# A hybrid decoder layer on one core: modulation pieces used one step after their load

## The chip, the cores and the metric

One core of one Trainium2 chip. The metric is the device time of one launch in microseconds (us), lower is better. The kernel before took 1296.67 us in the median of three runs (1293.77 to 1296.86).

## The reference

One layer of a decoder trunk on 256 tokens of width 2048, all in float32. A conditioning vector `c` gives six modulation vectors by one matrix-vector product; they shift, scale and gate the two sub-layers:

```
mod = (silu(c) @ w_ada + b_ada)                    # w_ada: 2048 x 12288, 96 MB
sh1, sc1, g1, sh2, sc2, g2 = split(mod, 6)
h = rms_norm(x, norm1_g) * (1 + sc1) + sh1
q, k, v, u = split(h @ w_in, ...)                  # w_in: 2048 x 4096
attn = dilated_attention(rms_norm(q), rms_norm(k), v)
y = gelu(s5_mixer(u, ...));  ssm = y * sigmoid(y @ w_glu + b_glu)
x = x + g1 * (concat(rms_norm(attn), rms_norm(ssm)) @ w_out)
h2 = rms_norm(x, norm2_g) * (1 + sc2) + sh2
return x + g2 * (square(relu(h2 @ w_ff1)) @ w_ff2) # w_ff1: 2048 x 8192, w_ff2: 8192 x 2048
```

## The kernel before, in words

**Weights.** Every large product is made in three matmuls of a reduced float32 form (`mm3`, lines 188 to 192): the weight is split into a high part `wh` (a copy on ScalarE, ACT) and a low part `wl` (a subtraction on VectorE, DVE), the activation likewise, and TensorE (PE) adds high by high, high by low and low by high. `load_w` (line 178) loads a block of 512 x 512 weights in two halves of 512 KB, each into one place of the tag `raw` (line 173), splits each and returns both. There are five places `raw` (`RAW = 5`), three `wh` and three `wl`. All loads are issued by one queue, SP, in order; a load waits there until a place of its tag is free, and a `raw` place comes free when the `wl` made from it is done.

**Modulation.** `w_ada` is read in 96 pieces of 1 MB (24 blocks of four). `ada_pieces` (line 238) loads a piece and uses it at once: for the eight blocks in `PE_BLOCKS` by small matmuls on PE (line 246), for the others by a product with a running sum on DVE (`stt`, line 155; two of 128 x 1024 a piece, one for each `raw` place). A piece goes into two `raw` places, or into a place of another tag that is idle at that time: `U`, `PD`, `WB0` (whole, 1 MB) or `T0` (two halves one after the other); `ring["tags"]` names the tags in turn, and `RINGS` holds their lists for six stretches of the program. T0 is also the place of tables and scratch of the state-space part.

**Order.** `pump(n)` (line 276) makes n pieces. `pump_at(i)` adds `PUMPS[i]` to a running sum and pumps the whole part of it; it is called after each part of the input projection (a part is one `load_w` with its 24 matmuls), after each column block of `w_out`, after the first parts of `w_ff1`, and in a few other places; `ff1` pumps one piece at its start, and the last four come in one call before the last `ff2`. `make_h` and `make_h2` need certain pieces to be complete. `PUMPS`, in the order of the program:

```
PUMPS = (2.5, 2.75, 1.0, 1.5, 0.75, 0.75, 1.5, 1.25, 1.0, 2.0, 0.25, 2.75, 1, 0.75)
run(w_in_block(0, [0]), 0) ... n in (6, 7): run(w_in_block(n, [0]), 1)   # kg 0: PUMPS 0, 1
run(w_in_block(2 + w, [0, 1]), 2); run(w_in_pair(4, [0, 1]), 3)          # PUMPS 2, 3
run(w_in_block(0 and 1, [1, 2]), 4); run(w_in_pair(6, [1, 2]), 5)        # PUMPS 4, 5
```

What the program text does not fix is fixed by a planner that runs when the kernel is built (`schedule_with_timeline_sim=True`): for each engine and for SP it takes, at each moment of a modelled run, the instruction that stands earliest in the program among those that could start. So the order on DVE is that in which the model expects loads to land; on the chip each engine then keeps this order.

**Names.** `tc.issue_after(ins)` puts what is traced inside it behind `ins` in the order of its engine, without a wait. A product of a piece is `raw<-raw,cbc` in the trace, a split `wh<-raw` (ACT, L158) and `wl<-raw,wh` (DVE, L133).

Of the kernel before, what the change touches and what calls it, by code (L numbers as in the profile page):

```python
# [1 line left out]

# [7 lines left out]
F32 = mybir.dt.float32  # L10
# [3 lines left out]
ALU = mybir.AluOpType  # L14
PSUM = bass.MemoryType.PSUM

P = 128
# [7 lines left out]
RQ = 4  # L25
NB = 512
RAW = 5
RINGS = (('raw',), ('raw',), ('T0', 'PD', 'raw', 'raw'), ('T0', 'raw', 'raw'), ('U', 'raw'), ('WB0', 'U', 'raw', 'raw'))
PUMPS = (2.5, 2.75, 1.0, 1.5, 0.75, 0.75, 1.5, 1.25, 1.0, 2.0, 0.25, 2.75, 1, 0.75)

COLS = {}
# [11 lines left out]
ADA_ORDER = (4, 0, 5, 1, 6, 2, 7, 3, 8, 9, 10, 11, 12, 16, 13, 17, 14, 18, 15, 19, 20, 21, 22, 23)  # L43
# [70 lines left out]
class _K:  # L114
    def __init__(self, nc, tc, I, out, pools):
        self.nc, self.tc, self.I, self.out = nc, tc, I, out
        self.sb, self.ps = pools
        self.n = 0

    def t(self, tag, shape, dt=F32, bufs=1):  # L120
        self.n += 1
        return self.sb.tile(list(shape), dt, name=f"{tag}_{self.n}", tag=tag, bufs=bufs)

# [4 lines left out]
    def tr(self):  # L128
        self.n += 1
        return self.ps.tile([P, NB], F32, name=f"tr_{self.n}", tag="tr", bufs=4)  # L130
# [7 lines left out]
    def add(self, out, a, b, eng=None):  # L138
        return self.tt(out, a, b, ALU.add, eng)
# [28 lines left out]

    def split(self, hi, lo, v):
        self.copy(hi, v)  # L170
        return self.sub(lo, v, hi.bitcast(F32))

    def raw(self, src, tag="raw"):
        raw = self.t(tag, [P, 2, NB], bufs=RAW if tag == "raw" else 1)
# [13 lines left out]
    def mm3(self, ps, xh, xl, wh, wl, start, stop):  # L188
        mm = self.nc.tensor.matmul
        mm(ps, xh, wh, start=start, stop=False)  # L190
        mm(ps, xh, wl, start=False, stop=False)  # L191
        mm(ps, xl, wh, start=False, stop=stop)  # L192


def _body(nc, tc, I, out, sb, ps):
    k = _K(nc, tc, I, out, (sb, ps))
    t, tr = k.t, k.tr
# [31 lines left out]
    def ada_raw(src):  # L229
        ring["i"] += 1  # L230
        tag = ring["tags"][ring["i"] % len(ring["tags"])]
        if tag not in ("raw", "T0"):
            raw = t(tag, [P, 4, NB])
            nc.sync.dma_start(raw, src.rearrange("p (a n) -> p a n", a=4))
            return [raw]
        return [k.raw(src[:, 2 * NB * i : 2 * NB * i + 2 * NB].rearrange("p (a n) -> p a n", a=2), tag) for i in range(2)]

    def ada_pieces(b):
        c4 = slice(4 * b, 4 * b + 4)
        if b in PE_BLOCKS:  # L240
            acc = tr()
            for g in range(4):
                q = 0
                for raw in ada_raw(I["w_ada"][b, g]):
                    for i in range(raw.shape[1]):
                        mm(
                            acc[32 * q : 32 * q + 32, :], cpad[:, 4 * g + q, :], raw[:, i, :],
                            start=g == 0, stop=g == 3,
                        )
                        q += 1  # L250
                if g < 3:
                    yield
            rows = t("rows", [P, NB], bufs=2)
            copy(rows, acc)
            pc = tr()
            for j in range(4):
                mm(pc[:, j : j + 1], rows[:, 128 * j : 128 * j + 128], ones, start=True, stop=True)
            add(mod[:, c4], pc[:, 0:4], col["b_ada"][:, c4])
        else:
            part = t("adap", [P, 2, 4], bufs=2)  # L260
            for j in range(4):
                o = 0
                for i, raw in enumerate(ada_raw(I["w_ada"][b, j])):
                    n = raw.shape[1] * NB
                    rf = raw.rearrange("p a n -> p (a n)")
                    stt(rf, rf, 1.0, cbc[:, o : o + n], ALU.mult, ALU.mult, accum=part[:, i, j : j + 1])
                    o += n
                if i:
                    add(part[:, 0, j : j + 1], part[:, 0, j : j + 1], part[:, 1, j : j + 1])
                if j < 3:  # L270
                    yield
            add(mod[:, c4], part[:, 0], col["b_ada"][:, c4])
        yield

    state = {"left": 96, "gen": None, "due": 0.0}

    def pump(n=1, until=None):
        while n > 0 and state["left"] > (96 - until if until is not None else 0):
            if state["left"] % 4 == 0:
                state["gen"] = ada_pieces(ADA_ORDER[24 - state["left"] // 4])  # L280
            next(state["gen"])
            state["left"] -= 1
            n -= 1

    # norm1
    rw = t("HB", [P, 4, SEQ])
    onek, sel = rw[:, 3, 0:32], rw[:, 3, P : 2 * P]
    nc.vector.memset(onek, 1.0 / DM)
# [15 lines left out]
    hs = {}  # L304

    def make_h(kg):
        hs[kg] = t("HA" if kg % 2 == 0 else "HB", [P, 2, 4, SEQ], F32R)
        c4 = slice(4 * kg, 4 * kg + 4)
        stt(g1c[:, c4], mod[:, 16 + 4 * kg : 20 + 4 * kg], 1.0, col["n1g"][:, c4], ALU.add, ALU.mult)
        for kc in range(4 * kg, 4 * kg + 4):  # L310
            v = xTf[:, kc]
            mul(v, v, rbc)
            nc.scalar.activation(v, v, AF.Identity, bias=mod[:, kc : kc + 1], scale=g1c[:, kc : kc + 1])
            end = k.split(hs[kg][:, 0, kc % 4], hs[kg][:, 1, kc % 4], v)
        return end.ins
# [152 lines left out]
            pr = slice(64 * gp, 64 * gp + 64)  # L468
            copy(dst(gp)[pr], src[pr])

    # state input tables: rows (s, gp, j), columns (gp, p)
    padB = t("PD", [P, 32, 2, 2, 16])
    padCs = [t(f"WB{i}", [P, 8, 2, 2, 4, 16]) for i in range(2)]
    cw = t("V", [P, 2, 2, 32, 16])
# [26 lines left out]
                nc.tensor.transpose(pt[:, P * e : P * e + P], src, ident)  # L501
            copy(wb[i][:, r : r + 2].rearrange("p r i n -> p (r i n)"), pt)

    # state output tables and the causal kernel inside a chunk
    def ca_step(d, X, Y, rr=slice(0, 32)):
        if d == 0:
            ts(c0[:, 1], c0[:, 1], -1.0, ALU.mult)
# [79 lines left out]

    s5_small()
    pump(8)
    h_end = make_h(0)  # L590
    ring["tags"] = RINGS[0]
    with tc.issue_after(rbc_end):
# [53 lines left out]
    for n in (6, 7):  # L646
        run(w_in_block(n, [3]), 8)

    # attention
    qk = accs["qk"]  # L650
    va = accs["v"]
    qss = t("qss", [P, 4, 32])
# [26 lines left out]
    def y_block(r8):  # L679
        pt = k.acc()  # L680
        pv = pt.rearrange("p (r c) -> p r c", r=8)
        for r in range(r8, r8 + 8):
            mm(pv[:, r - r8], toep[:, r].rearrange("p g s j -> p (g s j)"), u2[:, :, r, :], start=True, stop=False)
            for ri in range(2):
                for gp in range(2):
                    pr = slice(64 * gp, 64 * gp + 64)
                    mm(
                        pv[pr, r - r8], ca[pr, r, ri].rearrange("p s j -> p (s j)"), H[pr, ri, r, :],
                        start=False, stop=ri == 1,
                    )  # L690
        copy(yv[:, :, r8 : r8 + 8], pt.rearrange("p (r h c) -> p h r c", r=8, h=2))

    def att_scores(hp):
# [66 lines left out]
    def row_bcast(b0):  # L760
        g = t("PD", [P, 4, NB])
        for n in range(4):
            pg = tr()
            for j in range(4):
                c = b0 + 4 * n + j
                mm(pg[:, P * j : P * j + P], mod[:, c : c + 1].to_broadcast([P, P]), ident, start=True, stop=True)  # L766
            copy(g[:, n], pg)
        return g
# [59 lines left out]
        att_values(n)  # L828
    branch_rstd(sq2, 2)
    pump(99, until=48)  # L830
    g1b = row_bcast(32)
    x = t("XT", [P, 2, DM])
    nc.sync.dma_start(x, I["x"])

    # w_out
    zs = t("TO", [P, 2, DM])

    def w_out_half(half, xh, xl, n):
# [59 lines left out]

    def make_h2(kg):
        pump(99, until=56 + 8 * kg)  # L900
        c4 = slice(4 * kg, 4 * kg + 4)
        stt(g2c[:, c4], mod[:, 64 + 4 * kg : 68 + 4 * kg], 1.0, col["n2g"][:, c4], ALU.add, ALU.mult)
        for c in range(4 * kg, 4 * kg + 4):
            v = x1T[:, c]
            nc.scalar.activation(v, v, AF.Identity, bias=mod[:, 48 + c : 49 + c], scale=g2c[:, c : c + 1])
            k.split(h2h[:, c], h2l[:, c], v)

    # feed-forward
    y2 = [t("WB2", [P, DM]), t("WB3", [P, DM])]
    slots = [t(s, [P, 2, 4, SEQ], F32R) for s in ("V", "WB0", "HA", "U", "WB1", "HB")]  # L910
    xs = t("XT", [P, 2, 2, 4, SEQ], F32R)
# [68 lines left out]
    for G in range(4):  # L980
        if G < 3:
            aas[G + 1] = [ff1(G + 1, 0)]
        if G == 3:
            pump(99)
            g2b = row_bcast(80)
            for m in range(2):
                mul(y2[m], y2[m], g2b.rearrange("p n f -> p (n f)"))
                add(y2[m], y2[m], z[:, m])
        for n in range(4):
            ff2(G, n, aas[G], G == 3, g2b)  # L990
        if G < 3:
            aas[G + 1] += [ff1(G + 1, j) for j in range(1, 4)]
# [21 lines left out]
```

## Time and profile before

| | |
|---|---|
| runs | 1293.77, 1296.67, 1296.86 us |
| profiled execution | span 1291.1 us from its first to its last instruction; its whole time is not listed beside it, the median of the runs is 5.6 us above the span |
| busy | PE 1210.1, weight loads 947.5, DVE 873.3, ACT 595.8 us |
| read from memory | 296.31 MB, 231 GB/s over the span |

A page's busy shares are averages; the table of stretches (us from the span's start) says where an engine has room. A wait is put down to what ended it. Start times of PE's matmuls are the better measure of their pace, since their ends overlap.

### The profile page before, as it was taken

The page shows a single profiled execution, that of the slowest core. Times are in us where ns is not written, and L with a number is a line of the kernel's source. Part 1 is how long each engine was busy: PE and PEld are TensorE (multiplying, and loading weights), DVE is VectorE, ACT ScalarE, POOL GpSimd, SP SyncE. Part 2 cuts the span into 40 slices and gives each one's busy share as a digit, 9 for nine tenths or more (in the row PEclk, how much of TensorE's full clock was granted, in tenths as well). Part 3 has the DMA queues.
Part 4 walks back from the last instruction along what each step waited for, and adds up shares of the span by engine and source line. Part 5 has one row for each costly group of instructions (what it writes and reads, how often), then busy time and mean ns, then how long its engine had stood idle before and what let it go on. Part 6 is the DMA issues. An engine that isn't in the chain of part 4 may idle for free. (4 is left out here: it accounts for less than half of the span.)

```text
span 1291.1 us, 15788 instructions
## 1 busy us (share of the span) xinstructions
PE 1210.1 (94%) x5818; PEld 947.5 (73%) x5818; DVE 873.3 (68%) x1307; ACT 595.8 (46%) x820; POOL 41.3 (3%) x28
## 2 busy tenths in 40 slices
PE   5787999999999889699999999999999999998998
PEld 1356778866688667477788888888888888886886
DVE  9697678899658988765664456554666555667754
ACT  3579544322388434634454444443344433343432
POOL 3000000000000440000000000000000000000000
PEclk9687999998899999799999999999999999998999
DMA  9687898888726788487555576655667555677562
GB/s 332 234 280 269 332 350 307 291 311 294 260 84 207 239 268 281 156 267 247 193 182 192 189 253 211 217 184 188 224 216 248 185 186 186 224 245 258 176 217 95
DMA packets 80572, 299.44 MB, mean 232 GB/s; under 512 B 8944, under 2 KB 9200, under 8 KB 78576
## 3 DMA queue, kind: packets, MB, share of 16 engines
q1 hardware_dynamic: 80496, 298.45, 68.3%
q8 instruction: 45, 0.74, 0.2%
q14 instruction: 31, 0.25, 0.1%
HBM read 296.31 MB, written 2.10 MB: 231 GB/s over the span
## 5 line engine op out<-in xcount | busy, mean ns | idle before, releaser
L133 DVE TENSOR_TENSOR wl<-raw,wh 128x1024 fp32r<-128x1024 f32 x360 | 443.1, 1234 | 285.4 <-ACT wh L158 283.8
L158 ACT ACTIVATE wh<-raw 128x1024 fp32r<-128x1024 f32 x360 | 380.9, 1060 | 505.4 <-PE acc L192 370.1
L192 PE MATMUL acc<-wh,CA 128*128 128x512 f32 x512 | 204.4, 399 | 0.2 <-DVE CA L133 0.2
L155 DVE SCALAR_TENSOR_TENSOR raw<-raw,cbc 128x1024 f32<-128x1024 f32 x112 | 140.4, 1258 | 59.5 <-DMA raw<-w_ada 57.1
L191 PE MATMUL acc<-wl,TO 128*128 128x512 f32 x448 | 177.4, 396 | 1.4 <-DVE wl L133 1.4
L190 PE MATMUL acc<-wh,TO 128*128 128x512 f32 x448 | 161.9, 395 | 0.9 <-ACT rows L927 0.9
L192 PEld LDWEIGHTS acc<-wh,CA 128*128 128x128 f32 x512 | 97.4, 190 | 22.3 <-DVE CA L133 0.4
L192 PE MATMUL acc<-wh,HA 128*128 128x512 f32 x256 | 101.3, 398 | 0.0
L191 PEld LDWEIGHTS acc<-wl,TO 128*128 128x128 f32 x448 | 84.4, 188 | 21.4 <-DVE wl L133 2.0
L190 PEld LDWEIGHTS acc<-wh,TO 128*128 128x128 f32 x448 | 84.3, 188 | 20.3 <-ACT rows L927 1.1
L191 PE MATMUL acc<-wl,HA 128*128 128x512 f32 x192 | 77.4, 403 | 0.0
L190 PE MATMUL acc<-wh,HA 128*128 128x512 f32 x192 | 71.0, 404 | 6.5 <-ACT wh L158 6.5
L191 PE MATMUL acc<-wl,HB 128*128 128x512 f32 x192 | 76.2, 398 | 0.4 <-DVE wl L133 0.4
L192 PE MATMUL acc<-wh,HB 128*128 128x512 f32 x192 | 75.1, 393 | 0.0
L190 PE MATMUL acc<-wh,HB 128*128 128x512 f32 x192 | 69.8, 399 | 2.2 <-ACT HB L158 2.2
L192 PEld LDWEIGHTS acc<-wh,HA 128*128 128x128 f32 x256 | 48.6, 190 | 11.5 <-DVE T L133 0.8
L191 PE MATMUL acc<-wl,U 128*128 128x512 f32 x128 | 51.0, 398 | 2.5 <-DVE wl L133 2.5
L191 PE MATMUL acc<-wl,WB 128*128 128x512 f32 x128 | 51.4, 402 | 0.0
L192 PE MATMUL acc<-wh,WB 128*128 128x512 f32 x128 | 51.2, 400 | 0.0
L191 PE MATMUL acc<-wl,XT 128*128 128x512 f32 x128 | 50.8, 396 | 0.0
L192 PE MATMUL acc<-wh,XT 128*128 128x512 f32 x128 | 50.7, 396 | 0.0
L190 PEld LDWEIGHTS acc<-wh,HA 128*128 128x128 f32 x192 | 36.4, 191 | 17.5 <-ACT wh L158 9.5
(271 smaller groups left out, 1869.5 us busy)
## 6 DMA issues: line engine op xcount, KB each, us to landing
raw<-w_ff SPq DMA_DIRECT2D x256, 512.0 KB, 4.4
raw<-w_ada SPq DMA_DIRECT2D x158, 512.0 KB, 5.4
raw<-w_in SPq DMA_DIRECT2D x64, 512.0 KB, 5.5
raw<-w_out SPq DMA_DIRECT2D x32, 512.0 KB, 4.8
U<-w_ada SPq DMA_DIRECT2D x8, 1024.0 KB, 7.6
T<-w_ada SPq DMA_DIRECT2D x8, 512.0 KB, 6.2
raw<-w_glu SPq DMA_DIRECT2D x8, 512.0 KB, 5.6
PD<-w_ada SPq DMA_DIRECT2D x3, 1024.0 KB, 6.6
```

The source lines that it names most:

```text
L133: return (eng or self.nc.vector).tensor_tensor(out, a, b, op=op)
L155: self.nc.vector.scalar_tensor_tensor(out, a, s, b, op0=op0, op1=op1, accum_out=accum)
L158: self.nc.scalar.activation(out, a, AF.Copy, scale=scale)
L190: mm(ps, xh, wh, start=start, stop=False)
L191: mm(ps, xh, wl, start=False, stop=False)
L192: mm(ps, xl, wh, start=False, stop=stop)
```

## The change

A piece is now a generator of two steps: the first loads it, the second uses it. `pump` first uses what is pending (`drain`), and then for each of its n pieces again drains, loads the piece and leaves it pending; so of a call with n pieces all but the last are used within the call, and the last one by the next call, whatever its n. A use on DVE is put behind the last split traced so far, a use on PE behind the last main matmul traced so far (`mm3`, and the state output in `y_block`; the GLU's matmuls are not counted). `drain` also runs before a tile of the tags U, PD or WB0 is made, in `make_h` and `make_h2`, and before the two `row_bcast`. T0 is out of `RINGS`.

```diff
+PLACES = ("U", "PD", "WB0")
-RINGS = (('raw',), ('raw',), ('T0', 'PD', 'raw', 'raw'), ('T0', 'raw', 'raw'), ('U', 'raw'), ('WB0', 'U', 'raw', 'raw'))
+RINGS = (('raw',), ('raw',), ('PD', 'raw', 'raw'), ('raw',), ('U', 'raw'), ('WB0', 'U', 'raw', 'raw'))
...
     def t(self, tag, shape, dt=F32, bufs=1):
+        if self.drain and tag in PLACES:
+            self.drain()
...
     def split(self, hi, lo, v):
         self.copy(hi, v)
-        return self.sub(lo, v, hi.bitcast(F32))
+        r = self.sub(lo, v, hi.bitcast(F32))
+        self.last_split = r.ins
+        return r
...
-        mm(ps, xl, wh, start=False, stop=stop)
+        self.last_main = mm(ps, xl, wh, start=False, stop=stop).ins
...
+    def behind(name):
+        ins = getattr(k, name, None)
+        return tc.issue_after(ins) if ins is not None else contextlib.nullcontext()
...
+    def ada_piece(b, g):
         c4 = slice(4 * b, 4 * b + 4)
+        raws = ada_raw(I["w_ada"][b, g])
+        yield
         if b in PE_BLOCKS:
...
+            with behind("last_main"):
+                for raw in raws:
...
+            with behind("last_split"):
+                for i, raw in enumerate(raws):
...
+    pending = []
+
+    def drain():
+        while pending:
+            next(pending.pop(0))
 
     def pump(n=1, until=None):
+        drain()
         while n > 0 and state["left"] > (96 - until if until is not None else 0):
-            if state["left"] % 4 == 0:
-                state["gen"] = ada_pieces(ADA_ORDER[24 - state["left"] // 4])
-            next(state["gen"])
+            drain()
+            i = 96 - state["left"]
+            piece = ada_piece(ADA_ORDER[i // 4], i % 4)
+            next(piece)
+            pending.append(piece)
             state["left"] -= 1
             n -= 1
```

## Rows read from the trace of the kernel before

**Rows 1.** The page's busy time: us, share of the span, instructions.

```profile
PE 1210.1 (94%) x5818; PEld 947.5 (73%) x5818; DVE 873.3 (68%) x1307; ACT 595.8 (46%) x820; POOL 41.3 (3%) x28
```

**Rows 2.** Stretches: length, busy us (count) by engine, clock, DMA share, GB/s.

```profile
60.00:142.00 82.00, 69.17 (x366) 52.89 (x361) 67.06 (x122) 67.34 (x129) 1.82 (x1) 0.87 0.82 285
142.00:231.00 89.00, 88.62 (x396) 68.00 (x395) 68.14 (x98) 41.75 (x53) 0.22 (x1) 1.00 0.92 336
231.00:392.00 161.00, 156.82 (x1102) 121.33 (x1101) 129.82 (x234) 71.48 (x118) 0.00 (x0) 0.93 0.67 237
392.00:470.00 78.00, 67.96 (x325) 54.57 (x323) 67.47 (x123) 39.83 (x72) 20.09 (x12) 0.91 0.73 243
470.00:522.00 52.00, 48.13 (x216) 38.30 (x216) 44.43 (x56) 26.64 (x38) 8.29 (x4) 1.00 0.84 279
...
540.00:600.00 60.00, 54.94 (x229) 43.15 (x230) 39.14 (x62) 27.28 (x39) 0.00 (x0) 0.99 0.71 231
600.00:1163.00 563.00, 561.84 (x2480) 456.86 (x2479) 318.19 (x335) 242.64 (x263) 0.00 (x0) 1.00 0.63 208
1163.00:1200.00 37.00, 32.78 (x151) 26.11 (x150) 24.92 (x37) 14.14 (x18) 0.00 (x0) 0.91 0.78 260
```

**Rows 3.** Waits of the span: engine line, waited for, us, times, longest.

```profile
DVE raw L155 <- DMA raw<-w_ada: 57.1, 56, 3.9
...
PEld acc L191 <- DVE wl L133: 18.6, 16, 3.9
```

**Rows 4.** Waits of the queue SP, the whole span.

```profile
SPq L175 <- DVE wl L133: 673.0, 309, 17.5
```

**Rows 5.** Timeline 561 to 571: start, us, what [idle before <- what ended it].

```profile
561.94 1.06 ACT L158 ACTIVATE wh<-raw 128x1024 fp32r<-128x1024 f32 x1 [2.29 <-DMA raw<-w_ff]
...
567.53 1.23 DVE L155 SCALAR_TENSOR_TENSOR raw<-raw,cbc 128x1024 f32<-128x1024 f32 x1 [3.87 <-DMA raw<-w_ada]
...
568.68 1.22 DVE L133 TENSOR_TENSOR wl<-raw,wh 128x1024 fp32r<-128x1024 f32 x1
...
569.96 0.50 PE L191 MATMUL tr<-wl,TO 128*128 128x512 f32 x1 [2.54 <-DVE wl L133]
```

**Rows 6.** Timeline 438 to 451.

```profile
438.33 1.06 ACT L158 ACTIVATE wh<-raw 128x1024 fp32r<-128x1024 f32 x1 [1.38 <-PE acc L192]
...
449.11 2.35 DVE L133 TENSOR_TENSOR wl<-raw,wh 128x1024 fp32r<-128x1024 f32 x2
...
450.38 0.79 PE L191 MATMUL acc<-wl,CA 128*128 128x512 f32 x1 [3.21 <-DVE wl L133]
...
450.97 0.63 PE L192 MATMUL acc<-wh,CA 128*128 128x512 f32 x1
```

**Rows 7.** Timeline 682 to 689.

```profile
682.28 1.06 ACT L158 ACTIVATE wh<-raw 128x1024 fp32r<-128x1024 f32 x1 [1.66 <-PE acc L192]
683.37 1.23 DVE L133 TENSOR_TENSOR wl<-raw,wh 128x1024 fp32r<-128x1024 f32 x1 [1.49 <-ACT wh L158]
...
688.06 0.40 PE L191 MATMUL acc<-wl,V 128*128 128x512 f32 x1
```

**Rows 8.** DMA issues, 142 to 231: queue, count, KB each, median us to landing.

```profile
raw<-w_in SPq DMA_DIRECT2D x29, 512.0 KB, 5.5
```

**Rows 9.** DMA issues, 600 to 1163.

```profile
raw<-w_ff SPq DMA_DIRECT2D x198, 512.0 KB, 4.3
```

**Rows 10.** Timeline 50 to 90.

```profile
51.51 2.67 PE L246 MATMUL tr<-raw,cpad 128*32 128x512 f32 x8
...
57.37 1.09 PE L246 MATMUL tr<-raw,cpad 128*32 128x512 f32 x2
...
61.53 0.48 PE L190 MATMUL acc<-wh,HA 128*128 128x512 f32 x1
...
72.45 1.06 PE L246 MATMUL tr<-raw,cpad 128*32 128x512 f32 x8
73.54 0.92 SPq L175 DMA_DIRECT2D raw<-w_in  x2
...
85.24 0.39 PE L192 MATMUL acc<-wh,HA 128*128 128x512 f32 x1
86.60 0.48 PE L190 MATMUL acc<-wh,HA 128*128 128x512 f32 x1
```

More of the change, by code (lines that the diff above doesn't have):

```diff
@@ L1 @@
+import contextlib
 import math
@@ L117, in __init__ @@
         self.sb, self.ps = pools
+        self.drain = None
         self.n = 0
     def t(self, tag, shape, dt=F32, bufs=1):
+        if self.drain and tag in PLACES:
+            self.drain()
         self.n += 1
@@ L236, in ada_raw @@
         return [k.raw(src[:, 2 * NB * i : 2 * NB * i + 2 * NB].rearrange("p (a n) -> p a n", a=2), tag) for i in range(2)]
-    def ada_pieces(b):
+    def behind(name):
+        ins = getattr(k, name, None)
+        return tc.issue_after(ins) if ins is not None else contextlib.nullcontext()
+    accs_ada = {}
+    def ada_piece(b, g):
         c4 = slice(4 * b, 4 * b + 4)
+        raws = ada_raw(I["w_ada"][b, g])
+        yield
         if b in PE_BLOCKS:
[L241 to L244, printed above, removed]
+            if g == 0:
+                accs_ada[b] = tr()
+            acc = accs_ada[b]
+            q = 0
+            with behind("last_main"):
+                for raw in raws:
@@ L245, in ada_pieces @@
                     for i in range(raw.shape[1]):
-                        mm(
+                        k.last_ada = mm(
                             acc[32 * q : 32 * q + 32, :], cpad[:, 4 * g + q, :], raw[:, i, :],
                             start=g == 0, stop=g == 3,
-                        )
+                        ).ins
                         q += 1
[L251 to L255, printed above, removed]
@@ L256, in ada_pieces @@
-            for j in range(4):
-                mm(pc[:, j : j + 1], rows[:, 128 * j : 128 * j + 128], ones, start=True, stop=True)
-            add(mod[:, c4], pc[:, 0:4], col["b_ada"][:, c4])
-        else:
[L260 to L263, printed above, removed]
+            if g == 3:
+                rows = t("rows", [P, NB], bufs=2)
+                copy(rows, acc)
+                pc = tr()
+                for j in range(4):
+                    mm(pc[:, j : j + 1], rows[:, 128 * j : 128 * j + 128], ones, start=True, stop=True)
+                add(mod[:, c4], pc[:, 0:4], col["b_ada"][:, c4])
+        else:
+            if g == 0:
+                accs_ada[b] = t("adap", [P, 2, 4], bufs=2)
+            part = accs_ada[b]
+            o = 0
+            with behind("last_split"):
+                for i, raw in enumerate(raws):
@@ L264, in ada_pieces @@
                     n = raw.shape[1] * NB
                     rf = raw.rearrange("p a n -> p (a n)")
-                    stt(rf, rf, 1.0, cbc[:, o : o + n], ALU.mult, ALU.mult, accum=part[:, i, j : j + 1])
+                    stt(rf, rf, 1.0, cbc[:, o : o + n], ALU.mult, ALU.mult, accum=part[:, i, g : g + 1])
                     o += n
                 if i:
-                    add(part[:, 0, j : j + 1], part[:, 0, j : j + 1], part[:, 1, j : j + 1])
-                if j < 3:
-                    yield
@@ L272, in ada_pieces @@
-            add(mod[:, c4], part[:, 0], col["b_ada"][:, c4])
+                    add(part[:, 0, g : g + 1], part[:, 0, g : g + 1], part[:, 1, g : g + 1])
+                if g == 3:
+                    add(mod[:, c4], part[:, 0], col["b_ada"][:, c4])
         yield
-    state = {"left": 96, "gen": None, "due": 0.0}
+    state = {"left": 96, "due": 0.0}
+    pending = []
+    def drain():
+        while pending:
+            next(pending.pop(0))
     def pump(n=1, until=None):
+        drain()
@@ L278, in pump @@
         while n > 0 and state["left"] > (96 - until if until is not None else 0):
-            if state["left"] % 4 == 0:
-                state["gen"] = ada_pieces(ADA_ORDER[24 - state["left"] // 4])
-            next(state["gen"])
+            drain()
[3 more added lines that the diff above has]
+            pending.append(piece)
             state["left"] -= 1
             n -= 1
+    k.drain = drain
     rw = t("HB", [P, 4, SEQ])
@@ L306, in make_h @@
     def make_h(kg):
+        drain()
         hs[kg] = t("HA" if kg % 2 == 0 else "HB", [P, 2, 4, SEQ], F32R)
@@ L589, in _body @@
     pump(8)
+    drain()
     h_end = make_h(0)
@@ L686, in y_block @@
                     pr = slice(64 * gp, 64 * gp + 64)
-                    mm(
+                    k.last_main = mm(
                         pv[pr, r - r8], ca[pr, r, ri].rearrange("p s j -> p (s j)"), H[pr, ri, r, :],
                         start=False, stop=ri == 1,
-                    )
+                    ).ins
         copy(yv[:, :, r8 : r8 + 8], pt.rearrange("p (r h c) -> p h r c", r=8, h=2))
@@ L830, in _body @@
     pump(99, until=48)
+    drain()
     g1b = row_bcast(32)
@@ L900, in make_h2 @@
         pump(99, until=56 + 8 * kg)
+        drain()
         c4 = slice(4 * kg, 4 * kg + 4)
@@ L984, in _body @@
             pump(99)
+            drain()
             g2b = row_bcast(80)
```

## The prediction

> **What bounds the kernel now.** I read the page's busy line first: TensorE works 94% of the span [rows 1]. The table of stretches then says where the other 6% is: from 600 to 1163 us PE has 561.84 of 563 us, from 142 to 231 it has 88.62 of 89, and what idles is 60 to 142 (82 - 69.17 = 12.8 us), 392 to 470 (10.0), 470 to 522 (3.9), 540 to 600 (5.1) and 1163 to 1200 (4.2) [rows 2]; the first 60 us are not touched, since no split or main matmul is traced before their pieces and all their loads go through `raw` on both sides. So two kinds of stretch matter: idle ones, where a wait may go, and full ones, where a new wait would show at once. The list of waits names what the change aims at: VectorE stood 57.1 us behind `w_ada` loads, and PE stood 18.6 us (weight loads) behind `wl` [rows 3]. But the queue that loads shows another limit: SP waited 673 us, 309 times, for a `raw` place to come free from a `wl` [rows 4]. Five `raw` places of 512 KB feed weights and pieces alike.
>
> The waits that go: at 567.53 a piece's product waits 3.87 us for its load, and the `wl` whose `wh` started at 561.94 comes behind it at 568.68; PE stands 2.54 us [rows 5]. At 438.33 a `wh` is made, its `wl` comes at 449.11, and PE waits 3.21 us and runs its next matmuls at 0.63 instead of 0.40 us [rows 6, 7].
>
> **What the change does to the queue.** It neither adds nor removes an instruction that computes; loads keep their place in the traced order. From PUMPS: calls load 1 to 3 pieces, and only the last of a call is used a step later; its use stands on DVE behind the last split of the next part, or on PE behind its last main matmul. Until then it holds two of the five places. Four pieces (eight `T` loads) lose T0: PD takes one more, `raw` six loads more.
>
> I number the halves of weights W1, W2, ...; a part is two halves, 12 matmuls each, and FF shows the pace: 198 halves in 563 us, 2.84 us each (I use 2.8) [rows 2, 9]. `wh` takes 1.06 and `wl` 1.23 us, 2.3 together [rows 7]. Requests come as A A' W3 W4 B B' W5 W6. With five places request n waits for release n-5. Now the releases come A A' W3 W4, and the loads run ahead. After the change they come W3 W4 A A': B' takes W3's place, W5 takes W4's, W6 takes A's. While B loads and A is still held, four of five places hold pieces, and the next part's first weight is asked for only when the last part's last one is split. With PE full and three `wh`, W4 is split 2.3 us after PE ends W1 (F1). With L from issue to landing, W5 is ready at F1 + 2.3 + L + 2.3; PE wants it at F1 + 8.4. It is late by L - 3.8, and, when such steps follow each other, the loop (L + 2.3 + one product of 1.23) runs against 5.6: L - 2.0 more each. L is 4.3 in FF [rows 9] and 5.5 from 142 to 231 [rows 8]: 0.5 and 2.3, or 1.7 and 3.5 us. A piece on PE is freed later still, after PE's own W4 (F1 + 8.4) and a first half of about 0.6: W6 then is ready at 9.0 + 5.5 + 2.3 = 16.8 against 11.2, and about 1.1 of that is filled by the piece's own matmuls [rows 10]: 4.5 us.
>
> **The sum, by stretches.**
> - 60 to 142: pieces 8 to 11 are PE's. In the trace their matmuls (51.51, 57.37) run before the first main one at 61.53 [rows 10]. Now 9, 10 and 11 stand behind the last main of part 2, which ended at 85.2; they fill the places, and the `w_in` load of part 3, issued at 73.54, comes at about 87.5 instead. Part 3, which began at 86.60, could start at 87.5 + 4.3 + 2.3 = 94: 8 us later, 12 if the queue stays behind, 0 if all of it falls into the 12.8 idle us. I take 5, since ACT and DVE have other work here that moves forward.
> - 142 to 231: DMA engines are 92% busy and PE is full [rows 2]. Steps where a `raw` piece is pending and the next is loaded into `raw` are, by PUMPS and RINGS: 21-22, 30-31 (1.7 each), 24-25, 27-28 (on PE, 4.5 each), 33-34 (two pieces, two products more: 1.7 + 2.5 = 4.2) and 35-36 right behind it (3.5): 20 us at the most. None, if the planner finds other matmuls to put there. As PE falls behind, the DMA thins and L goes toward 4.3, which makes it 13. I take 9.
> - 231 to 392: U and `raw` alternate, so no two pieces meet in `raw`; only PE's lag holds them. PE has 4.2 us idle [rows 2]. 0 to 6, taken as 1.
> - 392 to 470: calls of three, three, two and three pieces. Two of three are used in the same call, so they may still stand in front of a `wl`, now only the next part's. The wait of rows 6 goes (its products are behind the split by the new edge): 3.2 us and some 14 matmuls at 0.2 extra, 6 us. Against it: T being the last split, W5 gets its place at T + 5 (after four products) and is ready at T + 12.3, while PE is done at T + 2.8; such a hole of 9.5 us a step is covered only where attention's matmuls fall into it. Between -9 and +6; both are of one size, so 0.
> - 470 to 522: one piece per four halves. The loop is two loads and two splits, 2 x 4.3 + 4.6 = 13.2 us a step; the stretch takes 52 / 4 = 13.0 already. +1, between -3.9 (its idle time) and +5.
> - 540 to 600: 0.5 for a first, 2.3 for a following step: pairs 73-74, 75-76-77, 78-79, 3.8 in all, against 5.1 idle us, which are waits like that of rows 5 and go. -1, between -5 and +4.
> - 600 to 1163: a piece stays pending through a whole `ff1`, once through four `ff2` more. Three places give a half every (4.3 + 2.3) / 3 = 2.2 us, under 2.8, and in the trace `wl` of 683.37 is read at 688.06, a lead of 3.5 us [rows 7]. 0; at most 15 steps x 0.5 = 7.
> - 1163 to 1200: the four last pieces come in one call either way. Their products no longer stand between splits, but free their places later. 0, plus or minus 4.
>
> Sum 5 + 9 + 1 + 0 + 1 - 1 = 15: 1291.1 + 15 = 1306 for the profiled execution. The runs' median is 5.6 us above that span, so 1311.7, said as 1312.
>
> The Trainium skill, DMA: Bandwidth & Descriptors, section Anatomy of one DMA, fits a transfer as about 2.0 us plus bytes over 436e9 per second, for GpSimd's path; for 512 KB that is an estimate of 3.2 us. By it L - 3.8 is below zero and only followers and PE's pieces cost. The trace disagrees with it for SP's loads beside others (4.3 and 5.5).
>
> **The rivals.**
> - A, the cover holds: `raw` is asked for early enough all the same, since PE has a lead of 3.5 us, and every wait like those of rows 5 and 6 goes: 9 of the 10 idle us from 392 to 470 and some 5 of the 9 from 470 to 600, with nothing lost early. 14 less than the median: 1283. For it: PE's waits stand right behind such products. Against: 673 us of SP's waits for places. It decides from L at or below 3.8 us in 142 to 231.
> - B, both sides cancel: the holes of 142 to 231 fall under 5 us and the gains after 392 come to the same: 1297. For it: the gains are the better shown ones.
> - C, L is short: loads among fewer others land in 3.2 us, as by that page. Then 142 to 231 has 2.2 + 2.2 + 1.9 + 1.2 = 7.5 at most, of which I count half, 4, and 60 to 142 counts 4: 1306. Against it: L is 4.3 even where SP has one load in 2.8 us.
>
> **Chances.** My forecast (1300 to 1332) 0.60, A 0.22, B 0.13, C 0.05. A measurement here can tell about 0.3%, 3.9 us, from no change. Faster is A, 0.22; no difference is B, 0.13; slower is the forecast and C, 0.65. 1283 to 1332 leaves out half of A and some 0.08 above; the bounds of all terms together would be 1275 and 1361.
>
> **What would show it.** Right: VectorE's wait behind `w_ada` well under 57 us after 470; PE below 87 us busy in what answers to 142 to 231, waiting for `wh`, and ACT there for `w_in`; the third part starting past 90 us; PE pieces freed late (SP waiting for `tr L246`'s line). Wrong: those two early stretches as long as now, or PE's idle time after 392 halved with nothing lost before.

## The result, and the profile after

The kernel after took 1362.94 us in the median (1361.21 to 1364.71) against 1295.22 for the one before on the same chip: a ratio of 1.054 (95% interval 1.049 to 1.059). It is slower by 68 us; the sum of the forecast was 15. The page's busy line of after, whose span is 1362.9 us:

```profile
PE 1223.6 (90%) x5818; PEld 955.6 (70%) x5818; DVE 867.4 (64%) x1304; ACT 595.5 (44%) x822; POOL 34.1 (3%) x28
```

The work is the same (5818 matmuls on both sides), but PE's share fell from 94% [rows 1] to 90%. The waits of the whole span (engine and line, what it waited for, us, times, longest):

```profile
ACT wh L163 <- DMA raw<-w_ff: 131.9, 59, 6.9
ACT wh L163 <- DMA raw<-w_in: 86.4, 34, 6.9
...
PEld acc L197 <- ACT wh L163: 69.0, 26, 14.4
...
ACT wh L163 <- DMA raw<-w_out: 41.0, 18, 10.7
PEld acc L198 <- DVE wl L138: 28.9, 27, 2.7
...
DVE raw L160 <- DMA raw<-w_ada: 6.6, 7, 1.8
```

The same waits in the kernel before:

```profile
ACT wh L158 <- DMA raw<-w_in: 36.6, 21, 5.0
ACT wh L158 <- DMA raw<-w_out: 28.2, 8, 10.6
...
ACT wh L158 <- DMA raw<-w_ff: 16.7, 6, 4.4
PEld acc L190 <- ACT wh L158: 15.5, 9, 4.6
```

VectorE's wait for `w_ada`, 57.1 us before [rows 3], is down to 6.6. In its place ACT waits for weights, and PE's weight loads wait 69.0 us for `wh`, once for 14.4 us. The late thing is no longer a piece but a weight. PE's wait behind `wl`, which the change was to take away, is not smaller over the whole span: 28.9 us after 18.6 [rows 3]. SP's list names what its loads wait for:

```profile
SPq L182 <- DVE wl L138: 719.1, 323, 15.6
SPq L182 <- DVE raw L160: 88.2, 81, 12.0
```

The first grew by 46 us from [rows 4]; the second is a place that waits for a piece's product. It is no larger in sum than before (93.1 us), but its longest wait is 12.0 us where 2.8 was. The table of stretches, cut where after has done the same work as at the marks of [rows 2] (first columns: start:end, length, PE's busy us):

```profile
60.00:153.00 93.00, 73.99 (x429) 56.74 (x430) 60.54 (x109) 66.64 (x129) 1.81 (x1) 0.87 0.67 236
153.00:264.00 111.00, 96.29 (x394) 71.35 (x393) 76.53 (x109) 41.99 (x54) 0.22 (x1) 0.94 0.81 281
264.00:428.00 164.00, 154.51 (x1109) 120.87 (x1108) 128.98 (x229) 69.58 (x117) 0.00 (x0) 0.95 0.64 234
428.00:528.00 100.00, 69.58 (x317) 56.39 (x315) 64.05 (x121) 46.28 (x77) 20.69 (x16) 0.83 0.57 193
528.00:583.00 55.00, 51.36 (x209) 40.08 (x210) 38.93 (x52) 21.52 (x32) 0.46 (x1) 0.91 0.69 225
605.00:665.00 60.00, 53.22 (x211) 41.08 (x211) 39.49 (x57) 19.88 (x19) 0.00 (x0) 0.94 0.75 254
665.00:1235.00 570.00, 565.12 (x2481) 455.69 (x2480) 313.27 (x333) 243.39 (x271) 0.00 (x0) 1.00 0.62 204
```

What was 78 us in w_out (392 to 470) is 100, with 30 us idle on PE where 10 were; 89 full us (142 to 231) are 111 with 15 idle. The other 8 us of that stretch are the matmuls themselves: 394 of them took 96.29 us where 396 took 88.62, at a granted clock of 0.94 instead of 1.00. Over the whole span PE idles 139.3 us (1362.9 - 1223.6) where it idled 81.0, which is 58 us more, and the same 5818 matmuls take 13.5 us longer, at a mean granted clock of 0.943 instead of 0.957. How much of that clock the holes brought about no run separates.

The largest hole, on VectorE (start, us, what):

```profile
445.06 1.23 DVE L138 TENSOR_TENSOR wl<-raw,wh 128x1024 fp32r<-128x1024 f32 x1 [0.49 <-ACT wh L163]
...
455.73 1.81 DVE L138 TENSOR_TENSOR HA<-rows,U 128x256 fp32r<-128x256 f32 x2
457.47 1.21 DVE L160 SCALAR_TENSOR_TENSOR raw<-raw,cbc 128x1024 f32<-128x1024 f32 x1
```

on SP, whose first row is two loads, the second of them issued at the end of the row's 12.73 us:

```profile
446.31 12.73 SPq L182 DMA_DIRECT2D raw<-w_ada  x2
459.86 9.28 SPq L182 DMA_DIRECT2D raw<-w_out  x4
```

and on PE:

```profile
467.58 1.22 PE L197 MATMUL acc<-wh,CA 128*128 128x512 f32 x2 [14.19 <-ACT wh L163]
```

I number the halves of the weights in the order of the program, as the prediction does; W73 is the first of w_out. W76's `wl` is done at 446.3. The pieces' products stand behind the last split traced, and that is attention's (`HA<-rows,U`, written by `att_values` through the same `split`), which comes at 455.73. Until 458.7 no product runs and no place comes free; W77's load is issued at 459.86, and PE stands 14.19 us. The clock adds to it (PEclk is the third number from the end):

```profile
440.00:453.00 13.00, 12.70 (x72) 10.71 (x71) 6.17 (x25) 11.15 (x24) 1.45 (x2) 1.00 0.11 40
453.00:467.50 14.50, 0.40 (x3) 0.19 (x1) 8.42 (x14) 3.34 (x7) 3.93 (x3) 0.62 0.42 141
467.50:471.00 3.50, 3.42 (x10) 2.87 (x11) 3.40 (x3) 2.14 (x3) 0.00 (x0) 0.50 0.34 94
471.00:480.00 9.00, 9.00 (x36) 7.28 (x36) 7.86 (x15) 4.28 (x7) 0.00 (x0) 0.86 0.76 255
```

Before the hole PE ran at 1.00 (2.4 GHz), behind it at 0.50 (1.2 GHz) and then at 0.86. My estimate from these rows is 0.5 x 3.5 + 0.14 x 9 = 3 us more.

### The profile page after: what moved, and what is told of

Read it like the earlier page. It is cut to its first block, busy times and chain, and to the rows that moved or that the text cites. A ratio compares the mean times of both kernels' runs of the same rounds, so it can differ in the third digit from the quotient of the medians.

```text
span 1362.9 us, 15710 instructions
## 1 busy us (share of the span) xinstructions
PE 1223.6 (90%) x5818; PEld 955.6 (70%) x5818; DVE 867.4 (64%) x1304; ACT 595.5 (44%) x822; POOL 34.1 (3%) x28
## 5 line engine op out<-in xcount | busy, mean ns | idle before, releaser
L199 PE MATMUL acc<-wh,HA 128*128 128x512 f32 x256 | 104.7, 412 | 0.0
L197 PE MATMUL acc<-wh,HA 128*128 128x512 f32 x192 | 73.5, 418 | 21.9 <-ACT wh L163 13.7
L198 PE MATMUL acc<-wl,HB 128*128 128x512 f32 x192 | 79.1, 412 | 5.6 <-DVE wl L138 5.6
L199 PE MATMUL acc<-wh,HB 128*128 128x512 f32 x192 | 77.9, 406 | 0.0
L197 PE MATMUL acc<-wh,HB 128*128 128x512 f32 x192 | 71.0, 408 | 6.8 <-ACT wh L163 6.8
L197 PEld LDWEIGHTS acc<-wh,HA 128*128 128x128 f32 x192 | 37.6, 199 | 33.7 <-ACT wh L163 17.2
L199 PEld LDWEIGHTS acc<-wh,HA 128*128 128x128 f32 x256 | 51.0, 199 | 11.4
L197 PE MATMUL acc<-wh,U 128*128 128x512 f32 x128 | 47.9, 413 | 7.8 <-ACT wh L163 7.8
L198 PE MATMUL acc<-wl,U 128*128 128x512 f32 x128 | 52.5, 410 | 1.4 <-DVE wl L138 1.4
L197 PEld LDWEIGHTS acc<-wh,HB 128*128 128x128 f32 x192 | 37.2, 197 | 19.9 <-ACT wh L163 10.2
```

The lines of the kernel that those rows point to most:

```text
L199: self.last_main = mm(ps, xl, wh, start=False, stop=stop).ins
```

## The experiments

**How they are read.** A tie is one of the two edges of the change (`behind`), and to defer a piece is to use it one step after its load. In each trace I take the time at which PE starts the first matmul of the second kind of a weight half (`xh` by `wl`, line 191 before and 198 after; four to a half, counted in order, and none in the GLU's halves 65 to 72), and subtract that of before's trace: this is the lag. The columns are what the lag grows by up to half 17 (143.0 us in before), 45 (227.6), 73 (399.4), 89 (472.0), 105 (536.4), 125 (601.3), 321 (1161.1), and the lag at the last one, 360. They answer to the stretches of the prediction: W17 to 60 to 142, W45 to 142 to 231, W73 to 231 to 392, W89 to 392 to 470, W105 and W125 to 470 to 600, and W321 to 600 to 1163.

```
                        W17   W45   W73   W89  W105  W125  W321 | W360
after                  11.0  21.8   2.8  22.0   3.2   4.2   6.8 | 71.8
e1  deferral only       0.2   9.4   0.5  -0.2  -1.1  -1.7   0.0 |  6.6
e2  ties only           1.0  15.0   0.9  15.3  -2.3  -5.7  -0.1 | 25.5
e3  rings only         -0.5   7.4   3.8  -0.4   0.2  -1.0   0.0 |  9.1
e7  no tie on PE        1.3  21.4   3.7  20.8   1.3   4.0   8.4 | 59.8
e8  no tie on DVE       0.9  10.2   4.6   0.7  -1.4   0.3   0.0 | 14.8
e10 tie as at load      0.6  12.1  -5.0  15.7  -2.4  -6.3  -0.1 | 14.0
e4  after, 6 places     3.7   9.3   8.7  16.2  -1.3  -4.8   0.7 | 32.1
e5  before, 6 places  -11.9   0.5  -1.0  -2.2   8.8  -2.8   0.8 |-12.5
e9  before, 4 places    9.7   6.8   5.3   7.7   5.7  -2.0   0.2 | 31.4
e6  weight's split     10.7  21.5   5.6  12.8   3.9   4.8   5.4 | 64.7
e13 w_out repaired     11.0  21.7   2.8  12.3   4.4   4.1   4.2 | 60.1
e16 w_out untied        8.8  21.8   2.3  19.1   3.1   3.6   5.3 | 63.4
e17 w_out tie alone     0.3   0.3   1.3   0.2  -2.1   1.0  -0.0 |  0.5
e18 untied early        0.1  11.4   3.1  20.2   2.1   5.2   6.4 | 48.1
e14 not deferred late  10.6  19.9   5.7  13.3  -3.1  -6.2  -0.1 | 39.1
e15 late tie alone     -1.5   0.5   9.9   0.3  -3.2  -6.4  -0.0 | -1.7
e11 6 places, tie 58+ -12.3   1.0   3.6   5.1  -2.9  -6.7   0.5 |-11.6
e12 6 places, tie 69+ -12.7   0.2   0.2  -2.6  -5.0  -6.3   0.5 |-24.0
```

Each row is one trace. In e15 the order of work on PE, VectorE, ACT and SP is that of before up to W88, and yet it shows 9.9 us in column W73. What differs there is the granted clock. From 320 to 340 us PE is busy throughout in both, at 0.84 with 218 matmuls in before and at 0.50 with 149 in e15:

```profile
320.00:340.00 20.00, 20.00 (x218) 13.42 (x217) 15.15 (x25) 6.37 (x8) 0.00 (x0) 0.84 0.67 238
320.00:340.00 20.00, 20.00 (x149) 13.41 (x152) 12.15 (x22) 4.25 (x6) 0.00 (x0) 0.50 0.47 167
```

So a single cell within 10 us of nothing is read only where other runs show it too.

**Deferral, ties, rings: one at a time (e1, e2, e3).**

```diff
 e1 (after):  behind(...) -> return contextlib.nullcontext()
 e2 (after):  pending.append(piece); + drain()
 e3 (before): RINGS of the kernel after
```

> The changed kernel without its two edges: a piece is still used by the next call, but not put behind the last split or the last main matmul. Places theory (pieces that are held in raw while the next ones load leave weights one place, and each part then waits for a load from its start): the planner may use a landed piece in any gap of DVE or PE, so the hold shrinks; 1300 to 1325 us. Order theory (the edges alone cost the time, since they put pieces and the modulation behind other work): 1295 to 1302. Delay theory (the use a step later costs by itself): 1350 or more.

> The changed kernel with the edges, but each piece is used in the call that loads it. Places theory: pieces go before the next part's weights land, two meet in raw only where PE frees them late; 1293 to 1312 us. Order theory: nearly all of the 68 us stay, 1345 or more. Delay theory: 1290 to 1300.

> The kernel before with the changed lists of places alone (no pieces through T0, one more through PD, six more loads into raw). Places theory: nothing is held longer, so little: 1295 to 1303 us. A theory that the lost place T0 itself is what costs from 142 to 231 us: 1315 or more.

Ratios: e1 1.003 (1.000 to 1.006), e2 1.019 (1.011 to 1.026), e3 1.009 (1.005 to 1.013). Of the theories, e1 fell into the range of the order theory, e3 into that of the places theory, and e2 into none of its three. Deferral without ties costs nothing that shows beside the rings: the order written on VectorE in w_out is that of before (below), as it would be if the planner puts an untied product where its model sees the load land, wherever it is traced. e1's own waits show it, 58.8 us as in [rows 3]:

```profile
DVE raw L160 <- DMA raw<-w_ada: 58.8, 55, 3.9
```

By the last column, deferral adds 6.6 - 9.1 = -2.5, the ties 25.5 - 9.1 = 16.4, the rings 9.1; that leaves 71.8 - 23.0 = 49 us to deferral and ties together. The medians give -4.6, 19.4, 9.6 and a rest of 43, so these parts are good to some 6 us.

**Which tie (e7, e8, e10).**

```diff
 e7 (after):  with behind("last_main")  -> with contextlib.nullcontext()
 e8 (after):  with behind("last_split") -> with contextlib.nullcontext()
 e10 (after): last_main, last_split read when the piece is loaded, not when it is used
```

> The changed kernel without the edge of the pieces on PE (behind the last main matmul); the edge on DVE stays. My priced terms put 5 us (60 to 142) and 9 of 142 to 231 on PE's pieces: 14 to 25 us come back before 260 us, nothing later: 1338 to 1350. If pieces on PE matter little, 1357 or more.

> The changed kernel without the edge of the pieces on DVE (behind the last split); the edge on PE stays. The loss after 390 us (33 us of it) has only DVE pieces, so it goes, and the early loss by PE's pieces stays: 1308 to 1328. If the DVE edge is harmless, 1355 or more.

> The change with its deferral and RINGS, but each piece's use is tied to the split or main matmul that was the last one when the piece was LOADED, not when it is used: so its place can come free before the next part's weights are asked for, and VectorE and TensorE still take it in a fixed order behind that part. Theory (places held across the next part are what costs): most of the change's loss goes, 1300 to 1325, with VectorE's waits for w_ada about as long as before. Rival (any order by hand costs, whatever it is tied to): 1345 or more.

Ratios: e7 1.046 (1.040 to 1.053), e8 1.010 (1.005 to 1.016), e10 1.010 (1.006 to 1.015). The loss before W17 (11.0) needs both ties and the deferral: it is 1.3 without PE's tie (e7), 0.9 without VectorE's (e8) and 1.0 with both ties and no deferral (e2). PE's tie makes no other loss, and e7 missed its range, 1338 to 1350: the 4.5 us a step that the prediction has for PE's pieces from 142 to 231 are not there (21.4 without the tie, 21.8 with it). VectorE's tie, with the deferral, makes nearly all the rest; of the 14.8 us that e8 keeps, 9.1 are there with the rings alone (e3). And not any tie does: with the same deferral and a tie to the split known at the load (e10), 58 of the 72 us go, while VectorE stays in a fixed order. In w_out that order is the one of e2, where nothing is deferred. I had expected VectorE's waits for `w_ada` to come back in e10, and they didn't; VectorE's tie alone takes them away. e8 and e10:

```profile
DVE raw L160 <- DMA raw<-w_ada: 63.8, 56, 4.1
DVE raw L160 <- DMA raw<-w_ada: 6.7, 7, 2.7
```

**Places (e4, e5, e9).** `cpad` in 48 columns instead of 512 makes room for a sixth `raw` place: the slices overlap, and the sum over `rows` then picks one row of every 32.

```diff
 e4 (after), e5 (before): RAW = 5 -> 6; cpad [P, 16, 32] -> [P, 48]; ones -> ident4[:, 0:1]
 e9 (before):             RAW = 5 -> 4
```

> The changed kernel with six raw places instead of five; the room comes from the padded column of c, kept in 48 columns instead of 512, so that the unused rows of a piece's result hold other sums, which a column of the identity leaves out when they are added up. Places theory: with six places the next part's first weight is asked for one split earlier (W5 takes the place of W3, not of W4), some 2.8 us a step, more than half of the loss comes back: 1310 to 1335 us. Order theory and delay theory: under 10 us come back, 1353 or more.

> Control for the run with six places: the kernel before with six raw places (the column of c kept in 48 columns in the same way). Places theory: the kernel before frees its pieces as soon as they land, so a sixth place helps only the waits for w_in and w_out loads; 0 to 15 us less, 1278 to 1293. If it gains some 40 us as well, six places say nothing about the change.

> The kernel before, unchanged but for four raw places in place of five: nothing is deferred, nothing is tied; it takes away lastingly about as much as one held piece half does. Theory (held places are what the change costs: a weight's first load waits for a place that a piece keeps): 10 to 35 us slower than before, 1300 to 1330, lost from 60 to 231 and from 392 to 600, and next to nothing from 600 to 1163, where three places already give a half every 2.2 us. Rival (places don't matter by themselves, the edges' order on VectorE and TensorE does): within 4 us of before, at most 1298.

Ratios: e4 1.020 (1.014 to 1.026), e5 0.994 (0.991 to 0.997), e9 1.020 (1.016 to 1.025). One place is worth 40 us to after and 12 to before (7 in the medians); taking one from before costs 31 (27 in the medians). In after the sixth place gives back 7.3 us up to W17, 12.5 in W45, 5.8 in W89 and 19.6 behind it, and W73 loses 5.9 more; the cells are single ones, their sum agrees with the medians. So the shortage of places shows early and late, but in w_out's first half 16.2 of the 22.0 us stay. ACT's wait for `w_ff` falls from 131.9 us to this in e4:

```profile
ACT wh L163 <- DMA raw<-w_ff: 73.5, 43, 4.5
```

**The first half of w_out, 392 to 470 (e6, e13, e16, e17, e18).**

```diff
 e6 (after):   last_split set in load_w only (a weight's, never attention's)
 e13 (e6):     + if 48 <= i < 59: drain()          # used in its own call
 e16 (after):  the same drain(), and no tie for pieces 48 to 58
 e17 (before): with tc.issue_after(last weight split) for pieces 48 to 58 alone
 e18 (after):  behind("last_split" if piece >= 48 else "")
```

> The changed kernel, but the last split is that of a weight alone: splits of the attention's values, of the GLU's output and of h no longer count. The first two w_out blocks are followed by attention, whose split comes some 10 us after the last weight's. If the edge to that split is what stretched the step from the first to the second w_out block (20.7 to 36.0 us), that step falls back to 20 to 24 us and the whole to 1344 to 1352. If held places alone stretch it, it stays at 30 or more and the whole at 1358 or more.

> The change with two repairs that act in w_out's first half alone: its eleven pieces (48 to 58) are used in the call that loads them, still behind the last split, and the last split is a weight's, never attention's. Theory (in 392 to 470 the change loses by two things and no third: the tie to attention's split, 15.4 us in four traces, and pieces held over a step): that stretch costs 0 plus or minus 4 in place of 22, the rest is as with the change, so the whole is 22 faster than it, 1335 to 1346. Rival (the order on VectorE by itself slows these steps): the stretch still costs 8 or more and the whole is 1350 or more.

> The change, but the eleven pieces of w_out's first half (48 to 58) are used in the call that loads them and are tied to nothing, as in the kernel before. New theory (in that stretch the tie itself costs, for a call's six loads then hold all five places until the last split, and the next weight is asked for 5 us after it; holding over a step and attention's split only add to it): 392 to 470 costs 0 plus or minus 4 in place of 22, and the whole is 1333 to 1348. Rival (a third thing in the change, the rings or the lag of 35 us, slows it): 8 or more stay there, 1350 or more.

> The kernel before with one edit: the eleven pieces of w_out's first half stand behind the last weight split, in the call that loads them; nothing is deferred, rings as before. New theory: this tie alone loses 9 to 16 us from 392 to 470, 1303 to 1311 in all, with the weight loads asked for some 5 us after a part's last split. Rival (the tie costs only behind the early loss): within 4 us of before.

> The change, but VectorE's pieces before w_out (up to 47) are tied to nothing; those from 48 on are tied and deferred as in the change, TensorE's ties too. It asks where the 22 us of 392 to 470 come from, after a tie there alone cost nothing (e17) and taking it away there alone gave 3 back (e16). Theory (the ties of the pieces before w_out decide it, by the state in which w_out is entered): 392 to 470 costs 0 to 6, 142 to 231 about 10 as without any of VectorE's ties, so some 16 at the start of w_out and 1315 to 1330 in all. Rival (ties and held pieces of the stretch itself, in either of which the other is enough): 392 to 470 costs 12 or more as in the change, 1332 to 1350.

Ratios: e6 1.050 (1.043 to 1.056), e13 1.043 (1.040 to 1.047), e16 1.047 (1.040 to 1.053), e17 0.998 (0.994 to 1.002), e18 1.039 (1.033 to 1.045). With attention's split out, the first step (W73 to W77) fell from 36.0 to 22.7 us as expected (before: 20.7), but the next took 23.4 where before took 14.1, and 12.8 of the 22 us stayed (e6). My theory that the tie to attention and the held pieces were all fell with e13 (12.3 stayed), the next, that the tie there is enough, with e17 (0.2), and e16 shows that 19 stay without tie and deferral in that stretch. e18 takes away VectorE's ties before w_out, and W73 then comes 14.5 us late instead of 35.6: the stretch still loses 20.2, with the same hole as in after. SP of e18:

```profile
425.23 12.74 SPq L182 DMA_DIRECT2D raw<-w_ada  x2
438.79 8.46 SPq L182 DMA_DIRECT2D raw<-w_out  x4
```

The order written on VectorE says what these have in common (Wn is the `wl` of half n, p a product of 128 x 1024, a one of attention's):

```
before, e1: W73 W74 p p W75 p p p p W76 W77 W78 p a a p p p W79 p a a p W80 W81 W82 p W83
e17:        W73 W74 W75 p p p p W76 p p a W77 W78 a p W79 p p p p a a p W80 W81 W82
after, e18: W73 W74 W75 a a W76 a a p p p p W77 W78 W79 a a p p p p W80 p p W81 W82 W83 W84
e13:        W73 W74 W75 a W76 p p p p a W77 W78 W79 W80 p p p a a p p p a a W81 W82 W83 W84
e16:        W73 W74 p p W75 a W76 a W77 W78 W79 a a p p W80 a a p p p p p p W81 W82 W83 W84
```

Where nothing is lost, four products or more stand ahead of W76's split and free their places for W77 to W79. In the others, three or four splits stand in a row and the products in a heap behind them, and the next weights wait for the heap. SP shows it: W77 is asked for 2.3 us after PE begins W73 in before (399.4) and 6.5 after it in e17 (401.3), but 24.9 after it in after and in e18, 10.8 in e13 and 9.7 in e16. Before and e17, the loads of W77 to W80:

```profile
401.68 5.97 SPq L175 DMA_DIRECT2D raw<-w_out  x4
407.77 5.39 SPq L176 DMA_DIRECT2D raw<-w_out  x4
```

In e16 the products aren't tied; the planner itself put them there, and on the chip their pieces had landed by 438.7 but were used from 463.41 on. VectorE of e16:

```profile
446.45 1.23 DVE L138 TENSOR_TENSOR wl<-raw,wh 128x1024 fp32r<-128x1024 f32 x1 [2.54 <-ACT wh L163]
452.31 1.24 DVE L138 TENSOR_TENSOR wl<-raw,wh 128x1024 fp32r<-128x1024 f32 x1 [3.53 <-ACT wh L163]
458.13 1.23 DVE L138 TENSOR_TENSOR wl<-raw,wh 128x1024 fp32r<-128x1024 f32 x1 [2.96 <-ACT wh L163]
463.41 1.22 DVE L160 SCALAR_TENSOR_TENSOR raw<-raw,cbc 128x1024 f32<-128x1024 f32 x1
```

and SP, where four weight loads take 17.84 us through the one place that is left:

```profile
441.87 17.84 SPq L182 DMA_DIRECT2D raw<-w_out  x4
```

So the heap is what costs, and the tie with the deferral is one way to it. e11 (below) is a weaker sign of the same: it has neither tie nor deferral ahead of piece 58, the last of this stretch. Up to W71 its order on VectorE is that of e5 and e12; then the planner puts the products behind W76 (W73 W74 W75 W76 p p p p a p a p W77). W77 is asked for 12.6 us after PE begins W73, where e5 and e12 ask for it 3.4 and 3.7 us ahead, and the first three steps take 56.7 us in place of 53.7 and 52.5. No run moves the products alone in the kernel after, so for its 22 us the heap is inferred from these orders. Why the planner's model makes one in e16 and e11 and not in e17 is open.

**Late (e14, e15) and better than both (e11, e12).**

```diff
 e14 (after):  + if i >= 59: drain()
 e15 (before): with tc.issue_after(last weight split) for VectorE's pieces from 69 on
 e11, e12 (e5): the same tie from 58 on, from 69 on
```

> The change, but from piece 59 on (w_out's second half, h2, feed-forward) each piece is used in the call that loads it, still tied. Theory (the same ties gain 8 us from 470 to 600 in e2, where nothing is deferred; held pieces turn that into the change's loss of 14 after 470): up to 470 as the change, +57, then -8 in place of +14: 1335 to 1350. Rival (the late loss comes from running late or from the rings): 1355 or more.

> The kernel before with five raw places; only VectorE's pieces from 69 on are tied behind the last weight split, nothing is deferred. It parts the 24 us that e12 gained into the sixth place and the late tie. Theory (they add up; the place gave 12 in e5's trace): 8 to 14 faster than before, 1281 to 1289. Rival (the tie gains only where a sixth place gives it slack): 1291 or more.

> The kernel before with the sixth raw place (cpad in 48 columns), and from piece 58 on (behind w_out) VectorE's pieces tied to stand behind the last weight split; no deferral, the old RINGS. It is the half of the change that e2 showed to gain 8 us late (470 to 600), without what costs early. Theory: 1274 to 1282 against 1284 for the sixth place alone. Rival (with six places the products no longer stand in the way of a split, or the planner used the freedom): 1283 to 1292.

> As the run beside it, but the tie begins only at piece 69 (h2 and feed-forward). Theory: the gain of the late edge is made from 540 to 600, so 1276 to 1284; if it is made in w_out's second half (470 to 522) this one has only the sixth place's, 1283 to 1287, and the other is below it.

Ratios: e14 1.029 (1.026 to 1.032), e15 0.994 (0.990 to 0.998), e11 0.988 (0.983 to 0.992), e12 0.978 (0.974 to 0.981). e14 came out below its forecast, 1332: behind W89 the deferral turns a gain of 9 into a loss of 14, and the ties without it do what the change set out to do. That gain is alike in six runs (W105 and W125 together: -8.0 in e2, -8.7 in e10, -9.3 in e14, -9.6 in e15, -9.6 in e11, -11.3 in e12). e12, 1269.35 us, came out below its forecast (1276 to 1284) and beats both kernels: the sixth place plus the tie in h2 and feed-forward. PE in its stretch from 522 to 600 has no idle time (62.37 of 78 us in before, 68.29 in e5):

```profile
522.00:600.00 78.00, 78.00 (x339) 63.27 (x339) 54.27 (x76) 37.07 (x48) 0.00 (x0) 1.00 0.76 263
```

e11 missed its gain: it loses 5.1 us in w_out, part of it ahead of its first tied piece (above), and all of it one trace's word.

## Why the prediction was wrong

The direction was right, and so was the mechanism as far as it goes (held places, a weight asked for too late); the size was off by 53 us, 68 against 15. The predicted terms and the lags: 5 and 11.0; 9 and 21.8; 1 and 2.8; 0 and 22.0; 1 and 3.2; -1 and 4.2; 0 and 6.8; 0 and 0.0.

- **The step that failed is "392 to 470 ... Between -9 and +6; both are of one size, so 0".** The working above it had the loop: W5's place at T + 5 and a hole of 9.5 us a step. Measured steps after the first are 19.1, 18.9 and 20.6 us (before: 14.1, 20.6, 17.2). The hole was then netted against a gain of 9, as if attention's matmuls would cover what was over. The gain came in part, since PE's idle time behind `wl` fell from 6.3 to 2.1 us, but holes behind `wh` took 22.4: 14.2, 4.3 and 4.0, at the start of the second, third and fourth step. Before (392 to 470) and after (428 to 528):

```profile
PE acc L191 <- DVE wl L133: 6.3, 3, 3.2
...
PE acc L197 <- ACT wh L163: 22.4, 3, 14.2
...
PE acc L198 <- DVE wl L138: 2.1, 2, 1.5
```

The order that takes the products out of the way of a `wl` is here the one that heaps them in front of the next load. And the upper bound of 6 left out attention: `last_split` is set in `split`, which attention calls too, so the first step took 36.0 us instead of 20.7 (15.4 of the 22 us, and 2 in e6, though its later steps lost more). A name's meaning was read off its use, not off all its callers.

- **142 to 231** was mis-sized: taken as 9 of at most 20, it measured 21.8. The 20 counted only pending pieces; the loss of T0 had been listed without a price, and e3 shows it at 7.4. e8 shows 10.2 without VectorE's tie, and so some 12 from the held pieces. That this is near the 9 taken is partly luck, since the two steps on PE, 9 of the 20, are not there (e7), and since some 8 of the 21.8 us are the same matmuls taking longer at a lower clock (0.94 for 1.00), which the sum counts nowhere as a cost. The landing time had the right size: for `raw<-w_in` in after's stretch (count, KB, median us) it is as in [rows 8]:

```profile
raw<-w_in SPq DMA_DIRECT2D x31, 512.0 KB, 5.5
```

- **60 to 142**: 5 taken, 12 as the bound, 11.0 measured. The forecast puts it down to PE's tie alone; e8 and e18 keep that tie and lose 0.9 and 0.1. Part 3 was not itself late by much; PE began it at 89.70 (86.60 in [rows 10]), and the loss is in its second half. PE's pieces before it and its start:

```profile
67.42 1.92 PE L263 MATMUL tr<-raw,cpad 128*32 128x512 f32 x16
...
77.02 2.82 PE L263 MATMUL tr<-raw,cpad 128*32 128x512 f32 x16
...
89.70 0.77 PE L197 MATMUL acc<-wh,HA 128*128 128x512 f32 x1
```

The pieces that ran at 51.51 and 57.37 before run here behind the first mains. SP's loads in that time:

```profile
78.54 0.86 SPq L182 DMA_DIRECT2D raw<-w_in  x2
79.88 10.58 SPq L182 DMA_DIRECT2D raw<-w_ada  x4
91.28 1.47 SPq L182 DMA_DIRECT2D raw<-w_in  x2
```

Part 3's loads are out at 78.54 (73.54 before) and not at 87.5, but the next ones at 91.28 (82.14 before).

- **470 to 600 and 600 to 1163**: forecast at 0 in sum, measured at 14.2, which comes from the deferral (e14: -9.4 for the same columns). I had counted a piece held through `ff1` as harmless because three places give a half every 2.2 us. They do on average, but ACT, which waited for no `w_ff` worth listing from 600 to 1163 before, waits for it 87.1 us in after, so that any further delay reaches PE. From 665 to 1235:

```profile
ACT wh L163 <- DMA raw<-w_ff: 87.1, 41, 6.3
```

The landing time fell there (4.3 in [rows 9]), which didn't help:

```profile
raw<-w_ff SPq DMA_DIRECT2D x195, 512.0 KB, 3.8
```

- **The range** (1283 to 1332) was too narrow: the terms are not independent, since one shortage of places pushes most of them towards their upper ends. That the bounds of all terms together, 1361, come so near to 1362.94 is luck: 22.0 stands against a bound of 6, and 2.8, 3.2 and 11.0 against 6, 5 and 12. The rivals with a gain (A) or none (B) failed on the same point; C's short landing is not seen. The estimate of 3.2 us by the Trainium skill (DMA: Bandwidth & Descriptors, Anatomy of one DMA), whose fit is for GpSimd's path, is met by SP's loads in neither stretch, 5.5 and 3.8 us.
- **What would show it**: VectorE's wait for `w_ada` well under 57 (6.6), ACT waiting for `w_in` where 142 to 231 was (52.3 us, 21.2 before), and PE's pieces freed late (SP behind them 62.6 us, 48.6 before) came true. PE below 87 us busy there did not as it is written, since the stretch grew: 96.29 us, which is 87% of 111 where it was nearly all of 89. The third part past 90 us was missed by 0.3.

## What to carry to other kernels

Where one ring of buffers feeds two streams, the order of the consumers is the order in which buffers come free: a rule that keeps stream A's work out of stream B's way delays B's next load by the whole heap of A, so write down releases and requests for a full period before pricing the wait that goes away. Holding a buffer "one step longer" and tying its use are each nearly free or cheap here (-2.5 and 16.4 us) and cost 43 to 49 more together. Terms that rest on one shared resource tend to their upper bounds together, so a range should reach towards the sum of them.

## What was not expected of the hardware

PE's granted clock was 0.50 in the 3.5 us behind a hole of 14.2 us in which PE did next to nothing, and 0.86 in the 9 us after that, with PE busy throughout: the price of such a hole was its length and some 3 us more. And a stretch can differ between two executions by as much as 9.9 us (e15 against before in 231 to 392) where the order on every engine is the same, which is more than many of the terms that were forecast. The granted clock was 0.50 for 20 us of it in one and 0.84 in the other, with PE busy throughout in both; why it stayed low in the one is open.
